# Two of three column blocks of a down projection by Strassen's seven products of quarters

## The chip, the cores and the metric

The kernel runs on one core of one Trainium2 chip. A core has a matrix engine (TensorE, "PE" in the profile, its weight loads "PEld"), VectorE ("DVE"), ScalarE ("ACT"), GpSimd ("POOL") and SyncE ("SP", which here only issues DMAs). They run side by side and meet at semaphores; each works through its own queue in order. 16 DMA engines move data between the chip's DRAM, where inputs and scratch arrays lie, and SBUF, the on-chip memory of 128 partitions. TensorE writes its results to PSUM, eight banks of 128 x 512 floats.

The metric is the device time of one execution in microseconds. Lower is better.

## What is computed

One step of a two-layer streaming encoder on 1024 prompt frames and 64 sample frames, 1088 columns in all, model width 1024, float32. Layer 0 mixes tokens by sliding-window attention, layer 1 by a diagonal state-space model (SSM). After either mixer comes the same gated feed-forward block (FFN), and the change is in its last product:

```python
def conv_ffn(h, prev, w_up, conv_w, conv_b, w_down):
    t = h.shape[1]
    up = h @ w_up                                   # 1024 -> 2 * 2816
    full = jnp.concatenate([prev.astype(up.dtype), up], axis=1)
    c = conv_b
    for j in range(CONV_WIDTH):                     # 3 taps, causal
        c = c + conv_w[j] * full[:, j:j + t]
    y = (jax.nn.gelu(c[..., :D_FF]) * c[..., D_FF:]) @ w_down   # 2816 -> 1024
    return y, full[:, -(CONV_WIDTH - 1):]
```

In each layer `x = x + rms_norm(conv_ffn(rms_norm(x)))` follows `x = x + rms_norm(mixer(rms_norm(x)))`.

## The kernel before

**Layout.** Activations are kept transposed: 128 channels on the partitions, frames along the columns. The 1088 columns fall into three blocks, 384, 384 and 320 (`BLK`). The inner size 2816 of the FFN is 22 tiles of 128 (`KF`), the width 1024 is 8 (`KD`).

**Matmuls in three.** A float32 product is made of three matmuls (`mm3`, L179). Each operand is split into a high part, a rounded copy made by ACT, and a low part, the difference made by DVE; low x high, high x high and high x low are added up in PSUM.

**Weights.** `wsrc` (L42 to L50) lists all weight units in order of use. `unit` (L149) hands out the next one and asks for those after it; `load_unit` (L161) loads a unit of 128 x 1024 floats into one of two `raw` buffers through SP's queue, ACT copies it (L175) and DVE subtracts (L176) into one of six buffers with the tag `big`. A unit of `w_down` holds two k-tiles of one half of the output (`mh`).

**The FFN** (`ffn`, L288). The up stage runs over 22 gated units `f`. Each makes two tiles of `up` (rows f and 22 + f) for all three blocks out of the normed input `h`, whose high and low parts fill the four buffers `blkA` and the two `blkB`. DVE takes the results from PSUM (L311), ACT and DVE make the convolution (L319 to L321), ACT the GELU (L334), DVE the product of the two (L337), and SP stores the gated tile to the scratch array `gd` in DRAM (L338, L340). The last three tiles of `up` before the very last are made together, block by block. In layer 0 the SSM's tables are prepared beside this at low priority (`side`, L342 to L349), in part on POOL and with a table in one of the two `ypA` buffers.

The down stage takes the blocks one after another. `part` loads gated tiles back from `gd` (`gr`) and splits them into `gt` (L385 on ACT, L386 on DVE), in two groups of 12 and 10 k-tiles (`KCUT`), in the buffers that `h` had. `down` makes 4 output tiles at a time, in 4 of the 6 PSUM banks with the tag `mm`; after the first group of k-tiles ACT copies the sums into `y` (L411), after the second DVE adds to it (L413). `y` lies in `ypA` for the first two blocks and in `ypB` for the third. When a block's `y` is whole, `after` makes its post-norm beside the next block's matmuls (`post_norm`, L260): ACT squares, DVE or POOL adds (L205, L280), DVE scales (L277), with loads of the residual `xl` and stores on SP's queue. In layer 0 more follows for the SSM: the next norm's squares, added on POOL for block 0, and scaled copies in four `blkA` buffers (`ssm_bounce`, L870), which `beside` starts at block 2.

**Order.** Instructions are not placed by hand. A scheduler orders each engine's queue at build time, from the order of the program as priority and its own model of durations; `order` and `later` bend this in places. Buffers of one tag are given out again when their last reader is done.

Of the kernel before, what the change touches and what calls it, by code (L numbers as in the profile page):

```python
# [8 lines left out]
F32 = mybir.dt.float32  # L9
# [20 lines left out]
GT = [[[(4, "blkA")] * 3, [(4, "blkA"), (3, "blkB"), (3, "blkB")]]] * 2 + [[[(4, "blkA")] * 3, [(4, "blkB"), (4, "blkB"), (2, "big")]]]  # L30
# [6 lines left out]
class Core:  # L37
    def __init__(self, ctx, tc, a):
# [5 lines left out]
        for i in range(2):  # L44
            self.wsrc += [("w_up", i, m + e) for m in range(KF) for e in (0, KF)]
            self.wsrc += [("w_down", i, k, mh) for _ in range(3) for c in range(2) for mh in range(2) for k in range(KCUT[c], KCUT[c + 1], 2)]
            if i == 0:
                self.wsrc.append(None)
                self.wsrc.append(None)
                self.wsrc += [("w_glu", m + e) for m in range(KD) for e in (0, KD)]  # L50
# [110 lines left out]
    def load_unit(self, src):  # L161
        nc = self.nc
        ap = self.a[src[0]]
        raw = self.wts.tile([P, D], F32, name="raw", tag="raw", bufs=2)
# [122 lines left out]

    def ffn(self, i, h, rb, after, side=None, beside=lambda: None):  # L288
# [6 lines left out]
        gd = self.dram.tile([P, KF, T], F32, name=f"gd{i}")  # L295

# [65 lines left out]
        def part(b, c):  # L362

            t0, n = BLK[b]
            k0 = KCUT[c]
            out = {}
            if (b, c) == (0, 0):

                r0 = [self.yp.tile([P, 6, n], F32, name="gr0", tag="yp" + x, bufs=y) for x, y in (("A", 2), ("B", 1))]
                for x, r in enumerate(r0):  # L370
                    nc.sync.dma_start(r, gd[:, 6 * x:6 * x + 6, t0:t0 + n])
            for sz, tag in GT[b][c]:
# [4 lines left out]
                for j in range(0, sz, 2):  # L377
                    e = min(2, sz - j)
                    if (b, c) == (0, 0):
                        x6 = (k0 + j) % 6  # L380
                        raw = r0[(k0 + j) // 6][:, x6:x6 + e]
                    else:
                        raw = self.t4([P, e, n], "gr")
                        nc.sync.dma_start(raw, gd[:, k0 + j:k0 + j + e, t0:t0 + n])
                    nc.scalar.activation(x[:, 0, j:j + e], raw, AF.Copy)  # L385
                    nc.vector.tensor_sub(x[:, 1, j:j + e], raw, x[:, 0, j:j + e].bitcast(F32))  # L386
                    for z in range(e):
                        out[k0 + j + z] = x, j + z
# [3 lines left out]
        def down(b, c, gs):  # L392
            t0, n = BLK[b]
            for mh in range(2):
                ps = [self.mm_ps() for _ in range(4)]
                ks = range(KCUT[c], KCUT[c + 1])
                ws = {k: self.unit(("w_down", i, k, mh)) for k in ks if k % 2 == 0} if (b, c, mh) == (2, 1, 1) else {}
# [10 lines left out]
                for m in range(4):  # L408
                    ym = y[b][:, 4 * mh + m]
# [5 lines left out]
        y = [None] * 3  # L415
        with self.boundary():
            for b in range(3):
                y[b] = self.bt(self.yp, b, "y")
                gs = part(b, 0)
                if b == 2:  # L420
                    gs.update(part(b, 1))
                    beside()
                down(b, 0, gs)
                if b < 2:
                    gs = part(b, 1)
                down(b, 1, gs)
                if b == 2 and i == 0:
                    self.wsrc.pop(0)
                after(b, y[b])
# [847 lines left out]
```

## Time and profile before

| | us |
|---|---|
| median of 3 runs | 2331.05 (2329.19 to 2331.17) |
| the profiled execution | 2330.36 |
| its span, first to last instruction | 2328.6 |
| attention and what lies ahead of it | 0 to about 400 |
| layer 0: FFN up, down | about 400 to 923, 923 to 1198 |
| layer 1: SSM with its output product | about 1198 to 1560 |
| layer 1: FFN up, down | about 1560 to 2050, 2050 to 2314 |

The profile is one execution, recorded by the hardware. The page gives for each engine the busy time and the share of the span; the granted clock tells how fast TensorE was allowed to run (1.00 is full). A row of a stretch reads: start:end, length, then for each engine the busy time and the number of instructions, the granted clock, the mean busy share of the 16 DMA engines and GB/s moved. A row of a group reads: line, engine, operation, out<-in, shape, count | busy us in all, mean ns of one | idle time of the engine just before, and what ended it. A row of the time line reads: start, length, engine, line, operation. A row of the chain of waits reads: start, length, what the end waited for there. A row of DMAs: out<-in, issuing queue, count, size, median us from issue to landing.

### The profile page before, as it was taken

The numbers are of one execution on the slowest core, as the hardware profiler recorded it, in microseconds if no ns is written. First come the engines' busy times: TensorE is split into PE (matmuls) and PEld (weight loads), VectorE is DVE, ScalarE is ACT, GpSimd is POOL, SyncE is SP. The second block draws the span as 40 slices with busy tenths as digits, with TensorE's granted clock in tenths as the row PEclk, the third lists the DMA queues.
The fourth block names the chain that finished last, engine by engine and source line by source line (L and its number), as shares of the span: only waits on it lengthen the run. The fifth ranks groups of instructions, "written<-read, shape, count | busy, mean of one in ns | idle before, by whom it ended". The sixth has DMA issues, their size and how long they took to land.

```text
span 2328.6 us, 35802 instructions
## 1 busy us (share of the span) xinstructions
PE 2262.8 (97%) x14259; PEld 2194.2 (94%) x14259; DVE 1437.8 (62%) x2596; ACT 948.4 (41%) x1735; POOL 281.6 (12%) x284
## 2 busy tenths in 40 slices
PE   8999999999999999999969899999999999999997
PEld 7987799999999999999967799999999999999997
DVE  8677639897576766564658712587555455465454
ACT  5256756422243333554435621443222222255343
POOL 6222006000123221010000000240000000000000
PEclk9999999999999999999988899999999999999998
DMA  5000015322234444755568721242211221165652
GB/s 192 34 30 19 19 60 173 115 70 104 94 121 141 133 140 144 245 178 178 187 222 284 226 66 49 71 163 84 95 64 68 84 75 65 56 211 182 214 180 97
DMA packets 167959, 287.02 MB, mean 123 GB/s; under 512 B 22032, under 2 KB 104496, under 8 KB 167664
## 3 DMA queue, kind: packets, MB, share of 16 engines
q1 hardware_dynamic: 157440, 273.41, 36.0%
q0 software_dynamic: 2032, 6.83, 0.9%
q10 hardware_dynamic: 8320, 4.49, 0.8%
q8 instruction: 112, 1.84, 0.3%
q14 instruction: 55, 0.45, 0.1%
HBM read 214.52 MB, written 70.17 MB: 122 GB/s over the span
## 4 chain that ended last, share of the span: by engine, by line
PE 49%; DMA 4%; DVE 3%; ACT 2%; issue 1%; POOL 0%; SPq 0%; ACTq 0%; DVEq 0%; POOLq 0%
PE mm L181 13%; PE mm L183 13%; PE mm L182 13%; DMA raw<-in_w_down 2%; PE pb L181 1%; PE pb L183 1%; PE pb L182 1%; PE pa L182 1%; PE pa L183 1%; PE pa L181 1%; DMA yd<-ys 1%; DVE whl L176 1%; DVE y L277 0%; ACT whl L175 0%; DMA gr<-gd 0%
## 5 line engine op out<-in xcount | busy, mean ns | idle before, releaser
L181 PE MATMUL mm<-hl,whl 128*128 128x384 f32 (+1 forms) x2232 | 735.1, 330 | 9.2 <-ACT whl L175 7.2
L182 PE MATMUL mm<-hh,whl 128*128 128x384 f32 (+1 forms) x2232 | 735.4, 329 | 0.0
L183 PE MATMUL mm<-hh,whl 128*128 128x384 f32 (+1 forms) x2232 | 732.9, 329 | 0.6 <-DVE whl L176 0.6
L175 ACT ACTIVATE whl<-raw 128x1024 fp32r<-128x1024 f32 x256 | 269.9, 1058 | 680.8 <-PE mm L183 557.5
L176 DVE TENSOR_TENSOR whl<-raw,whl 128x1024 fp32r<-128x1024 f32 x256 | 319.1, 1249 | 238.1 <-ACT whl L175 237.7
L181 PEld LDWEIGHTS mm<-hl,whl 128*128 128x128 f32 x2232 | 420.3, 188 | 11.2 <-ACT whl L175 7.2
L183 PEld LDWEIGHTS mm<-hh,whl 128*128 128x128 f32 x2232 | 420.0, 188 | 1.5 <-DVE whl L176 1.4
L182 PEld LDWEIGHTS mm<-hh,whl 128*128 128x128 f32 x2232 | 420.6, 188 | 0.4
L181 PE MATMUL mm<-gt,whl 128*128 128x384 f32 (+1 forms) x1056 | 346.1, 328 | 2.8 <-ACT y L411 1.8
L182 PE MATMUL mm<-gt,whl 128*128 128x384 f32 (+1 forms) x1056 | 345.5, 327 | 0.0
L183 PE MATMUL mm<-gt,whl 128*128 128x384 f32 (+1 forms) x1056 | 343.2, 327 | 0.5 <-DVE whl L176 0.5
L311 DVE TENSOR_TENSOR u<-rb,mm 128x384 f32<-128x384 f32 (+1 forms) x264 | 131.9, 507 | 273.8 <-PE mm L183 273.4
L181 PEld LDWEIGHTS mm<-gt,whl 128*128 128x128 f32 x1056 | 198.2, 188 | 3.7 <-ACT y L411 2.4
L183 PEld LDWEIGHTS mm<-gt,whl 128*128 128x128 f32 x1056 | 198.0, 188 | 0.8 <-DVE whl L176 0.8
L182 PEld LDWEIGHTS mm<-gt,whl 128*128 128x128 f32 x1056 | 198.3, 188 | 0.0
L320 DVE SCALAR_TENSOR_TENSOR t<-u,ppt,t 128x1090 f32<-128x1090 f32 x88 | 121.4, 1380 | 10.9 <-ACT t L319 8.2
L321 DVE SCALAR_TENSOR_TENSOR t<-u,ppt,t 128x1090 f32<-128x1090 f32 x88 | 119.8, 1361 | 1.7
L319 ACT ACTIVATE t<-u,ppt 128x1090 f32<-128x1090 f32 x88 | 114.3, 1299 | 11.0 <-DVE t L321 5.7
L280 POOL TENSOR_TENSOR y<-y,xl 128x768 f32<-128x768 f32 (+1 forms) x16 | 30.0, 1874 | 571.6 <-DVE y L277 517.0
L334 ACT ACTIVATE t<-t 128x1090 f32<-128x1090 f32 x44 | 49.0, 1114 | 100.4 <-DVE t L321 100.4
L1110 DVE SCALAR_TENSOR_TENSOR y<-pa,ppt,sg 128x384 f32<-128x384 f32 (+1 forms) x24 | 14.1, 594 | 95.2 <-ACT sg L1109 95.2
L386 DVE TENSOR_TENSOR gt<-gr,gt 128x768 fp32r<-128x768 f32 (+2 forms) x70 | 58.0, 865 | 11.8 <-ACT gt L385 11.6
(321 smaller groups left out, 3317.9 us busy)
## 6 DMA issues: line engine op xcount, KB each, us to landing
raw<-in_w_down SPq DMA_DIRECT2D x132, 512.0 KB, 4.0
raw<-in_w_up SPq DMA_DIRECT2D x88, 512.0 KB, 3.3
gd<-t SPq DMA_DIRECT2D x44, 512.0 KB, 2.6
pm<-prm SPq DMA_DIRECT2D x32, 522.0 KB, 7.4
gr<-gd SPq DMA_DIRECT2D x28, 384.0 KB, 5.0
xl<-x SPq DMA_DIRECT2D x24, 384.0 KB, 3.8
raw<-in_w_glu SPq DMA_DIRECT2D x16, 512.0 KB, 4.4
gr<-gd SPq DMA_DIRECT2D x22, 320.0 KB, 4.4
```

The lines of the kernel that those rows point to most:

```text
L175: nc.scalar.activation(w[:, 0], raw, AF.Copy)
L176: nc.vector.tensor_sub(w[:, 1], raw, w[:, 0].bitcast(F32))
L181: nc.tensor.matmul(out, w[:, 0, sl], xl, start=start, stop=False)
L182: nc.tensor.matmul(out, w[:, 0, sl], xh, start=False, stop=False)
L183: self.last_mm = nc.tensor.matmul(out, w[:, 1, sl], xh, start=False, stop=stop)
L280: x = by[q].tensor_add(yq, yq, xs[q])
L311: nc.vector.tensor_mul(u[:, t0 + 2:t0 + 2 + np_], rb[:, t0:t0 + np_], ps[:, :np_])
L319: nc.scalar.activation(t, u[:, 0:T + 2], AF.Identity, bias=cb(m), scale=cw(0, m))
L320: nc.vector.scalar_tensor_tensor(t, u[:, 1:T + 3], cw(1, m), t, op0=ALU.mult, op1=ALU.add)
L321: nc.vector.scalar_tensor_tensor(t, u[:, 2:T + 4], cw(2, m), t, op0=ALU.mult, op1=ALU.add)
L334: nc.scalar.activation(ta, ta, AF.Gelu_apprx_tanh)
L386: nc.vector.tensor_sub(x[:, 1, j:j + e], raw, x[:, 0, j:j + e].bitcast(F32))
```

## The change

In each layer, the down product of the first two blocks is made as one product of a 2 x 2 matrix of quarters by another (Strassen's scheme in Winograd's form). The inner size is halved to two times 11 k-tiles (`KH`), the output to two halves of 512, the columns to blocks 0 and 1. Seven products of quarters stand in place of eight. The first two and the fifth use quarters of `w_down` as they are, the other four use sums of quarters; four of the seven use sums of gated quarters.

Those sums are made during the up stage, one k-tile for each gated unit: for f = 1 to 11 of weight quarters (`sums_w`, stored to `sd`), for f = 11 to 21 of gated quarters (`sums_g`, stored to `td`). Each loads its quarters through POOL's DMA queue into a buffer `jt` (one of `ypA`), makes four additions there on GpSimd, and stores the result. A weight unit of a product has up to two k-tiles of one quarter (six units for 11 k-tiles). Each product has its own 11 split gated tiles; the first product's are loaded ahead into `yp` buffers. The results are added into `y` by DVE (the first product's copied by ACT), 4 tiles for each product, 8 for the sixth. Block 0 is whole after the fifth product and block 1 after the seventh. The third block is made as before.

```diff
-GT = [[[(4, "blkA")] * 3, [(4, "blkA"), (3, "blkB"), (3, "blkB")]]] * 2 + [[[(4, "blkA")] * 3, [(4, "blkB"), (4, "blkB"), (2, "big")]]]
+GT = [[(4, "blkA")] * 3, [(4, "blkB"), (4, "blkB"), (2, "big")]]
+KH = KF // 2
+PRODUCTS = (("a", 0, 0, 0, 0), ("a", 1, 0, 1, 0), ("s", 0, 0, 1, 1), ("s", 0, 1, 0, 1), ("a", 1, 1, 1, 0), ("s", 1, 1, 0, 0), ("s", 1, 0, 1, 1))
+SUMMED = (0, 0, 1, 1, 1, 1, 0)
...
-            self.wsrc += [("w_down", i, k, mh) for _ in range(3) for c in range(2) for mh in range(2) for k in range(KCUT[c], KCUT[c + 1], 2)]
+            self.wsrc += [("w_part", i, k) + x[:3] for x in PRODUCTS for k in range(0, KH, 2)]
+            self.wsrc += [("w_down", i, k, mh) for c in range(2) for mh in range(2) for k in range(KCUT[c], KCUT[c + 1], 2)]
...
+        if src[0] == "w_part":
+
+            _, i, k, s, kc, mh = src
+            n = min(2, KH - k)
+            if s == "s":
+                ap = self.sd[:, k:k + n, kc, mh]
+            else:
+                k += KH * kc
+                ap = self.a["w_down"][i, k:k + n, :, 512 * mh:512 * mh + 512].rearrange("k p m -> p k m")
+            raw = raw[:, :512 * n]
+            self.loaded = nc.sync.dma_start(raw.rearrange("p (k m) -> p k m", k=n), ap)
+            w = self.big([P, 2, D], "whl")[:, :, :512 * n]
+            nc.scalar.activation(w[:, 0], raw, AF.Copy)
+            nc.vector.tensor_sub(w[:, 1], raw, w[:, 0].bitcast(F32))
+            return w
...
+        sd = self.sd = self.dram.tile([P, KH, 2, 2, 512], F32, name=f"sd{i}")
+        td = self.dram.tile([P, KH, 2, 2, 384], F32, name=f"td{i}")
+
+        def sums(x, q, src, dst, weights):
+
+            nc.gpsimd.dma_start(x, src)
+            a11, a12, a21, a22 = q
+            G = nc.gpsimd
+            if weights:
+                G.tensor_add(a22, a21, a22)
+                G.tensor_sub(a21, a11, a21)
+                G.tensor_sub(a11, a22, a11)
+                G.tensor_sub(a12, a12, a11)
+            else:
...
+            nc.gpsimd.dma_start(dst, x)
...
+            if f == 1:
+                jt = self.yp.tile([P, 3072], F32, name="jt", tag="ypA", bufs=2)
+            if 1 <= f <= KH:
+                sums_w(jt, f - 1)
+            if f >= KH:
+                sums_g(jt, f - KH)
...
+            for sz, tag in ((4, "blkA"), (4, "blkA"), (3, "blkB")):
+                x = self.blk.tile([P, 2, sz, 384], F32R, name="gt", tag=tag, bufs=4 if tag == "blkA" else 2)
+                for j in range(0, sz, 2):
+                    e, k = min(2, sz - j), len(out)
+                    if p == 0:
+                        raw = r0[k // 6][:, k % 6:k % 6 + e]
+                    else:
+                        raw = self.t4([P, e, 384], "gr")
+                        nc.sync.dma_start(raw, td[:, k:k + e, kc, b] if SUMMED[p] else gd[:, KH * kc + k:KH * kc + k + e, 384 * b:384 * b + 384])
+                    split_units(x, slice(j, j + e), raw)
+                    out += [(x, j + z) for z in range(e)]
+            return out
+
+        def product(p, gs, ps):
+            ws = {}
+            two = lambda ks: [(k, m) for u in ((0, 1), (2, 3)) for k in ks for m in u]
+
+            for k, m in two(range(4)) + [(k, m) for k in range(4, KH - 3) for m in range(4)] + two(range(KH - 3, KH)):
+                if k - k % 2 not in ws:
+                    ws[k] = self.unit(("w_part", i, k) + PRODUCTS[p][:3])
+                w, (x, j) = ws[k - k % 2], gs[k]
+                o = k % 2 * 512 + m * P
+                self.mm3(ps[m][:, :384], w, slice(o, o + P), x[:, 0, j], x[:, 1, j], k == 0, k == KH - 1)
+
+        def pair(y0, y1, done):
+
+            lo0, hi0, lo1, hi1 = ([y[:, j + m] for m in range(4)] for y in (y0, y1) for j in (0, 4))
+
+            ends = ([(lo1, None)], [(lo0, lo1)], [(lo1, lo1)], [(hi1, lo1)], [(hi0, hi1)], [(hi1, hi1), (lo1, lo1)], [(lo1, lo1)])
+            for p in range(7):
+                gs = operand(p)
+                ps = [self.mm_ps() for _ in range(4)]
+                product(p, gs, ps)
+                for m in range(4):
+                    for o, x in ends[p]:
+                        if x is None:
+                            nc.scalar.activation(o[m], ps[m][:, :384], AF.Copy)
+                        else:
+                            nc.vector.tensor_add(o[m], x[m], ps[m][:, :384])
+                if p in (4, 6):
+                    done(p // 6)
...
         with self.boundary():
...
+            y = [self.bt(self.yp, b, "y") for b in range(2)]
+            pair(*y, lambda b: after(b, y[b]))
+            y = self.bt(self.yp, 2, "y")
+            gs = part(0)
+            gs.update(part(1))
+            beside()
+            down(y, 0, gs)
+            down(y, 1, gs)
+            if i == 0:
+                self.wsrc.pop(0)
+            after(2, y)
```

More of the change, by code (lines that the diff above doesn't have):

```diff
@@ L162, in load_unit @@
         nc = self.nc
+        raw = self.wts.tile([P, D], F32, name="raw", tag="raw", bufs=2)
+        if src[0] == "w_part":
[12 more added lines that the diff above has]
+            return w
         ap = self.a[src[0]]
-        raw = self.wts.tile([P, D], F32, name="raw", tag="raw", bufs=2)
         if src[0] == "w_down":
@@ L360, in ffn, with split_units, operand @@
                 pass
-        def part(b, c):
-            t0, n = BLK[b]
+        def split_units(x, u, raw):
+            nc.scalar.activation(x[:, 0, u], raw, AF.Copy)
+            nc.vector.tensor_sub(x[:, 1, u], raw, x[:, 0, u].bitcast(F32))
+        def operand(p):
+            _, _, _, kc, b = PRODUCTS[p]
+            out = []
+            if p == 0:
+                r0 = [self.yp.tile([P, 6, 384], F32, name="gr0", tag="yp" + x, bufs=y) for x, y in (("A", 2), ("B", 1))]
+                for x, r in enumerate(r0):
+                    n = min(6, KH - 6 * x)
+                    nc.sync.dma_start(r[:, :n], gd[:, 6 * x:6 * x + n, :384])
+            for sz, tag in ((4, "blkA"), (4, "blkA"), (3, "blkB")):
+                x = self.blk.tile([P, 2, sz, 384], F32R, name="gt", tag=tag, bufs=4 if tag == "blkA" else 2)
+                for j in range(0, sz, 2):
+                    e, k = min(2, sz - j), len(out)
+                    if p == 0:
+                        raw = r0[k // 6][:, k % 6:k % 6 + e]
[5 more added lines that the diff above has]
+            return out
@@ L365, in part @@
+        def part(c):
+            t0, n = BLK[2]
             k0 = KCUT[c]
             out = {}
[L367 to L372, printed above, removed]
+            for sz, tag in GT[c]:
                 if tag == "big":
@@ L377, in part @@
                 for j in range(0, sz, 2):
[L378 to L387, printed above, removed]
+                    raw = self.t4([P, 2, n], "gr")
+                    nc.sync.dma_start(raw, gd[:, k0 + j:k0 + j + 2, t0:])
+                    split_units(x, slice(j, j + 2), raw)
+                    for z in range(2):
                         out[k0 + j + z] = x, j + z
@@ L390, in part, with down @@
             return out
-        def down(b, c, gs):
-            t0, n = BLK[b]
+        def down(y, c, gs):
+            n = BLK[2][1]
             for mh in range(2):
@@ L396, in down @@
                 ks = range(KCUT[c], KCUT[c + 1])
-                ws = {k: self.unit(("w_down", i, k, mh)) for k in ks if k % 2 == 0} if (b, c, mh) == (2, 1, 1) else {}
+                ws = {k: self.unit(("w_down", i, k, mh)) for k in ks if k % 2 == 0} if (c, mh) == (1, 1) else {}
                 todo = [(k, m) for m in range(4) for k in ks] if ws else [(k, m) for k in ks for m in range(4)]
@@ L408, in down @@
                 for m in range(4):
-                    ym = y[b][:, 4 * mh + m]
+                    ym = y[:, 4 * mh + m]
                     if c == 0:
@@ L413, in down @@
                         nc.vector.tensor_add(ym, ym, ps[m][:, :n])
-        y = [None] * 3
         with self.boundary():
[L417 to L429, printed above, removed]
+            y = [self.bt(self.yp, b, "y") for b in range(2)]
[9 more added lines that the diff above has]
+            after(2, y)
     def attention(self, h, rb, after):
```

12 lines of the change are left out of this document (added).

## The prediction

> **What bounds the kernel now.** I read the page first, then the busy time of each engine in stretches cut at the kernel's stages (FFN of layer 0: up 380 to 923, down 923 to 1198; layer 1: up 1560 to 2050, down 2050 to 2314).
>
> ```profile
> PE 2262.8 (97%) x14259; PEld 2194.2 (94%) x14259; DVE 1437.8 (62%) x2596; ACT 948.4 (41%) x1735; POOL 281.6 (12%) x284
> ```
> ```profile
> core 0: us, PE busy (x) PEld busy (x) DVE busy (x) ACT busy (x) POOL busy (x), PEclk, DMA share, GB/s
> 380.00:923.00 543.00, 541.57 (x3341) 539.98 (x3340) 395.52 (x823) 193.08 (x284) 111.64 (x90) 1.00 0.37 121
> 470.00:560.00 90.00, 90.00 (x548) 90.00 (x547) 82.32 (x268) 25.50 (x39) 1.23 (x1) 1.00 0.26 88
> 923.00:1015.00 92.00, 91.66 (x525) 91.34 (x524) 56.21 (x66) 45.98 (x59) 0.93 (x3) 1.00 0.65 203
> 1015.00:1108.00 93.00, 93.00 (x541) 92.93 (x540) 50.68 (x59) 42.77 (x57) 11.33 (x7) 1.00 0.58 182
> 1108.00:1198.00 90.00, 84.36 (x565) 82.29 (x563) 57.64 (x69) 38.83 (x55) 4.15 (x5) 1.00 0.50 160
> 1200.00:1326.00 126.00, 92.30 (x880) 75.44 (x880) 100.97 (x186) 73.93 (x208) 5.87 (x40) 0.82 0.88 284
> 1560.00:2050.00 490.00, 489.58 (x2973) 489.52 (x2972) 263.68 (x389) 134.51 (x200) 0.39 (x1) 1.00 0.22 77
> 2050.00:2141.00 91.00, 91.00 (x524) 91.00 (x523) 50.46 (x53) 44.32 (x55) 0.61 (x1) 1.00 0.63 203
> 2141.00:2234.00 93.00, 93.00 (x538) 92.96 (x538) 47.37 (x55) 41.89 (x54) 4.16 (x2) 1.00 0.62 193
> 2234.00:2314.00 80.00, 80.00 (x548) 79.95 (x546) 39.43 (x50) 32.69 (x46) 3.99 (x2) 1.00 0.47 151
> ```
> In both FFNs PE is busy for all but a few us at full granted clock. The down rows (one for each block of columns) show it best: 91 and 93 us of PE for the blocks of 384 in layer 1, with DVE at about half and the DMA engines at 0.63. So PE sets the time there, and a matmul left out is time gained as long as nothing else grows past PE. Only block 2 of layer 0 (1108 to 1198) has a hole, 5.6 us.
>
> **The gain.** Blocks 0 and 1 issue 2 blocks x 22 k-tiles x 8 output tiles x 3 matmuls = 1056 matmuls of 384 columns in each layer; seven products issue 7 x 11 x 4 x 3 = 924. 132 go. Price of one, start to start: 91.00 us / 524 = 0.174, 91.66 / 525 = 0.175, 93.00 / 538 = 0.173. 132 x 0.174 = 23.0 us in a layer, **46 us** in both. [...]
>
> **What each product asks of the other engines.** A product takes 132 x 0.174 = 23.0 us of PE, and needs 5 weight units of 2 k-tiles and one of 1, 11 unit tiles split in two, and 4 sums out of PSUM (8 in the sixth product; the first product's 4 copies go to ACT).
>
> ```profile
> L176 DVE TENSOR_TENSOR whl<-raw,whl 128x1024 fp32r<-128x1024 f32 x256 | 319.1, 1249 | 238.1 <-ACT whl L175 237.7
> L175 ACT ACTIVATE whl<-raw 128x1024 fp32r<-128x1024 f32 x256 | 269.9, 1058 | 680.8 <-PE mm L183 557.5 <-DMA raw<-in_w_down 96.6 <-PE mm L485 11.9
> L386 DVE TENSOR_TENSOR gt<-gr,gt 128x768 fp32r<-128x768 f32 x40 | 37.0, 953 | 2.8 <-ACT gt L385 2.7
> L385 ACT ACTIVATE gt<-gr 128x768 fp32r<-128x768 f32 x40 | 31.8, 834 | 8.6 <-DMA gr<-gd 4.4 <-PE mm L181 2.1 <-PE mm L183 2.0
> L413 DVE TENSOR_TENSOR y<-y,mm 128x384 f32<-128x384 f32 x32 | 17.0, 554 | 4.5 <-PE mm L183 4.5
> ```
> DVE: 5.5 x 1.25 + 5.5 x 0.95 + 4 x 0.55 = 14.3 us of 23.0 (before, the same count of matmuls had 5.5 units, 2.75 splits and 2 sums: 10.6). ACT: 5.5 x 1.06 + 5.5 x 0.83 = 10.4. Both lie beside PE: 0 us. The sums out of PSUM leave 2 spare banks of 6, and the order of the first 4 and last 3 k-tiles gives the first two banks 18 + 24 matmuls = 7.3 us to be emptied, against 4 x 0.55 at most; 0 us.
>
> **Supply of weights.** This is the tightest cover. A raw buffer is filled, copied by ACT, subtracted by DVE, and filled again; there are two. The chain of waits in block 2 of layer 0 shows one round, and below it the landing times in layer 1's block 1:
>
> ```profile
> 1119.59 5.16 DMA raw<-in_w_down
> ...
> 1124.83 1.07 ACT whl L175
> ...
> 1125.92 1.24 DVE whl L176
> ...
> 1127.17 4.39 DMA raw<-in_w_down
> ```
> ```profile
> DMA to landing us min/median/max: 3.7/4.1/7.1
> ```
> A round is the landing L plus 2.4, so a product's six units take (5 x (L + 2.4) + L + 1.2) / 2 = 3L + 6.6. At L = 4.1: 18.9, under 23.0; the two meet at L = 5.5. L will rise: a product moves 2.88 MB of weights and 11 x 0.197 = 2.16 MB of units, 5.04 MB, where the same matmuls before moved 2.88 + 1.08 = 3.96; share 0.63 becomes about 0.80. One end: L stays at 4.1, no cost. Other end: the row with share 0.88 and its loads.
>
> ```profile
> pm<-prm SPq DMA_DIRECT2D x32, 522.0 KB, 7.4
> gr<-gd SPq DMA_DIRECT2D x28, 384.0 KB, 5.0
> prm<-tab POOLq DMA_DIRECT2D x16, 276.0 KB, 4.7
> ```
> On the line from (0.63, 4.1) to (0.88, 7.4), 0.80 gives 6.3: 25.5 us a product, 14 x 2.5 = 35 us lost. But `pm` loads are issued in bunches and queue behind each other. 1.08 MB more at 203 GB/s / 0.63 = 320 GB/s is 3.4 us a product, 0.6 on each load: L = 4.7, 20.7 us, still covered. Operand loads stand in SP's queue ahead of weight loads and single loads reach 7.1, so I take **5 us** for both layers, near the lower end.
>
> **The sums on GpSimd.** In each layer 44 additions of 512 and 44 of 384 elements, and 44 DMAs on POOL's own queue. A round (load, four additions, store) comes with each gated unit, 490 us / 22 = 22.3 us apart (two at f = 11).
>
> ```profile
> L644 POOL TENSOR_TENSOR m<-tq,tp 128x576 f32<-128x576 f32 x8 | 9.4, 1177 | 0.6
> L641 POOL TENSOR_TENSOR m<-tq,tp 128x576 f32<-128x576 f32 x8 | 14.5, 1816 | 295.6 <-DVE w L646 150.6 <-DVE u L300 145.1
> L843 POOL DMA_DIRECT2D prm<-tab x16 | 12.4, 775 | 2.4 <-POOL tab L841 2.4
> ```
> ```profile
> 1040.03 1.84 POOL L280 TENSOR_TENSOR y<-y,xl 128x768 f32<-128x768 f32 x1 [3.35 <-ACT whl L175]
> ```
> ```profile
> 1038.06 1.22 DVE L176 TENSOR_TENSOR whl<-raw,whl 128x1024 fp32r<-128x1024 f32 x1
> 1040.04 2.91 DVE L176 TENSOR_TENSOR whl<-raw,whl 128x1024 fp32r<-128x1024 f32 x1 [0.76 <-ACT whl L175]
> ```
> I estimate 1.15 us for one addition from the undisturbed 576-element row: 88 x 1.15 + 44 x 0.78 = 135 us of POOL in 490. POOL has the room, but it isn't alone: the last two rows are the same DVE subtraction, and beside a POOL addition it took 2.91 in place of 1.22, later by nearly the whole 1.84. L641 likewise takes 1816 ns where L644, the same shape, takes 1177. So the two engines hold each other up, one whole instruction at a time. The Trainium skill (SBUF — State Buffer, "SBUF: two separate sides") says this as a rule: a DVE instruction with two SBUF inputs and a GpSimd one that reads SBUF lock the shared ports for their whole length. It speaks against the change, and these rows agree.
>
> Price: at the worst each addition costs DVE its full 1.15, 101 us in a layer. Layer 1: 264 + 101 = 365 of 490. Layer 0: 396 + 101 = 497 of 543. Tight is only 470 to 560, where DVE has 82.3 of 90: 3.6 rounds x 4 x 1.15 = 17 us against 7.7 idle leaves DVE 9 us late. PE has six banks of 24 x 0.174 = 4.2 us each, so DVE can be some 20 us late with the products before PE stops. I take 0; the other end is 9 us, once. If that cover were gone, every us late would be one of PE.
>
> **Start of the down product.** The last round of unit sums can begin only when the last gated unit is stored.
>
> ```profile
> L181 PE MATMUL mm<-gt,whl x1056: 302/336/440, 923.8 to 2313.6; 128*128 128x384 f32 x118, 128*128 128x320 f32 x58
> ```
> ```profile
> 940.89 6.29 DMA gd<-t
> ```
> Stored at 947.2; POOL's load 4.7 (like `prm<-tab`): 952; four additions of 1.0 to 1.8: 956 to 959; store 4.7: 961 to 964; `gr` load 5.0 and split 1.8: 968 to 971. The third product, the first to read sums, starts at 923.8 + 46 = 970 and needs k-tile 10 only after 96 matmuls, at 987: 15 us to spare. What waits behind it: POOL's in-order queue holds nothing that is needed sooner, but the sums' buffer is wanted by block 0's `y` for the second product's results at 970: 6 us to spare. At the same time DVE works off the last gates without a pause, and two rounds of additions fall there: 0 to 8 x 1.0 us in each layer, I take 1 each, **2 us**.
>
> **Block 0's norm**, which lay beside 93 us of block 1, comes beside the last two products, 46 us.
>
> ```profile
> L277 DVE TENSOR_TENSOR y<-y,pr 128x768 f32<-128x768 f32 x24 | 21.3, 949 | 6.7 <-PE pr L233 6.7
> L205 DVE TENSOR_TENSOR sqa<-sqa 128x768 f32<-128x768 f32 x24 | 23.2, 969 | 22.6 <-ACT sqa L203 22.3
> ```
> DVE: 2 x 14.3 + 2.2 (the sixth product's second sums) + about 10 of norm (4 x 0.95, 4 x 0.97, 2 x 0.95) = 41 of 46. Its four loads of `xl` and its stores, 3.1 MB, stand in SP's queue among the weight loads there: (2 x 5.04 + 3.1) MB at 320 GB/s is 41 us of 46, so it is in these two products that I expect most of the 5 us. On DVE, layer 0 has POOL adding squares there too, 11.3 us of POOL in the row 1015 to 1108, so up to 52 of 46: 6 us late, carried into block 2, whose row leaves DVE 32 us free. I take 0, other end 6. The 5.6 us hole of that block may close or stay: -5.6 to 0, I take 0.
>
> **Sum**, from the profiled execution's 2330.36 us (span 2328.6 and 1.8 around it; 0.7 under the median 2331.05): 2330.4 - 46 + 5 + 2 = **2291.4**.
>
> **Rivals.**
> (a) Slower than before: weight landings become the bound outright. Place: the seven products; deciding point: 14 x (3L + 6.6 - 23.0) = 46, L = 6.6. At the longest landing of the row, 7.1, a product takes 27.9 us, 14 x 4.9 = 69 lost: 2330.4 - 46 + 69 = 2353. For: the rows at share 0.88. Against: medians of 4.1 at 0.63. Chance 0.07.
> (b) The same supply, in part: L = 6, 24.6 us a product, 22 lost, and 2 at the start: 2308. Chance 0.15.
> (c) The lock between POOL and DVE reaches PE at its upper ends, 9 in the up stage of layer 0 and 16 at the two starts: 2330.4 - 46 + 5 + 25 = 2314. For: the 2.91 row. Against: PE waits for no DVE work in either up stage, and the banks cover. Chance 0.10.
> (d) The last round of sums lands 10 us later than worked out, 4 past the spare, in both layers: 2299. Chance 0.05.
> (e) It saves nothing: 924 matmuls cost what 1056 did if one took 0.174 x 8 / 7 = 0.199 us. Nothing in the rows moves the price of one shape. 2330. Chance 0.03.
>
> **How the numbers follow.** The forecast as summed has 0.60, and its time is the prediction. Low end: all costs nothing and the hole closed, 2330.4 - 46 - 5.6 = 2279. High end: the supply at its upper bound, 2330.4 - 46 + 35 = 2319; (b), (c) and (d) lie within, (a) and (e) do not. About 0.2%, 5 us, is what a measurement of this kernel can tell from no change. Faster by more: 0.60 + 0.15 + 0.10 + 0.05 = 0.90; within: (e), 0.03; slower: (a), 0.07.
>
> **What would show it.** Right: the two-block stretch falls from 184 to about 162 us in each layer, PE without idle time in it, landings of `raw` under 5.5, and up stages as long as before though DVE's L176 and L320 grow. For (a) and (b): ACT's L175 waiting for `raw` while PE waits for L175, products longer than 23 us at unchanged matmul price. For (c): PE idle before an up matmul that waits for DVE. For (d): PE idle at the third product, released through `gr<-td` or `y`. For (e): start-to-start of a 384-column matmul above 0.174. Wrong altogether would be a longer stage that no row here touches, such as the SSM between 1200 and 1326.

## The result and the profile after

| | before | after |
|---|---|---|
| median, 4 runs each on one chip | 2330.63 us (2329.19 to 2331.17) | 2346.07 us (2343.43 to 2349.30) |
| ratio, 95% interval | | 1.0071, 1.0058 to 1.0083 |
| span of the profiled execution | 2328.6 | 2344.8 |
| mean granted clock | 0.986 | 0.978 |

The change makes the kernel 0.7% slower, by 15 us, where 39 us less had been predicted. Stage lengths, from PE's first and last matmuls of each stage in the two traces (up: from the last matmul of attention or of the SSM's output product to the first of the down product):

| us | up, layer 0 | down, layer 0 | SSM | up, layer 1 | down, layer 1 | what is left |
|---|---|---|---|---|---|---|
| before | 552.8 | 273.6 | 325.7 | 527.3 | 263.5 | 14.7 |
| after | 602.5 | 248.4 | 325.2 | 539.7 | 241.1 | 16.8 |
| | +49.7 | -25.2 | -0.5 | +12.4 | -22.4 | +2.1 |

So the seven products gave 47.6 us, and the stages in which their sums are made took 62 back, 50 of them in layer 0. First the engines on the page of after, then its busy times by stretches (start:end, length, each engine's busy time and instructions, granted clock, DMA share, GB/s):

```profile
PE 2237.7 (95%) x13995; PEld 2165.0 (92%) x13995; DVE 1565.7 (67%) x2652; ACT 954.2 (41%) x1743; POOL 625.5 (27%) x548
```

```profile
core 0: us, PE busy (x) PEld busy (x) DVE busy (x) ACT busy (x) POOL busy (x), PEclk, DMA share, GB/s
380.00:973.00 593.00, 558.82 (x3343) 554.61 (x3343) 467.01 (x826) 195.80 (x285) 273.73 (x210) 0.97 0.52 174
440.00:480.00 40.00, 36.96 (x207) 36.70 (x206) 39.56 (x75) 13.02 (x20) 17.70 (x13) 0.91 0.59 210
470.00:560.00 90.00, 90.00 (x547) 90.00 (x546) 88.43 (x243) 19.81 (x30) 39.43 (x33) 1.00 0.50 180
700.00:800.00 100.00, 93.00 (x572) 92.24 (x572) 72.16 (x99) 33.18 (x46) 50.76 (x39) 0.97 0.52 169
973.00:1136.00 163.00, 162.91 (x936) 161.76 (x935) 117.78 (x150) 87.50 (x113) 30.34 (x22) 1.00 0.81 265
1575.00:2087.00 512.00, 506.55 (x3066) 505.29 (x3065) 297.86 (x406) 140.05 (x212) 144.78 (x117) 1.00 0.41 142
2087.00:2249.00 162.00, 162.00 (x930) 161.56 (x929) 113.50 (x136) 85.50 (x110) 18.51 (x14) 1.00 0.83 270
```

The two stretches with the products, 973 to 1136 and 2087 to 2249, are full: 936 matmuls in 163 us and 930 in 162 (the products need 924), 0.174 each. The loss stands in the first row. Before, 3341 matmuls of this stage kept PE busy for 541.57 us of 543; now 3343 take 558.82 of 593. PE stands still for 34 us in place of 1.4, and the same matmuls are 17 us longer busy at a mean granted clock of 0.97: stops cost twice, once as time and once as clock after them.

What ended the idle time, in the view of waits from 400 to 974 of after (engine, line, waited for: us in all, times, longest), and then PE's only row of the same kind before:

```profile
POOL jt L323 <- DMA gd<-t: 69.4, 8, 17.6
POOL jt L327 <- DMA jt<-in_w_down: 57.2, 10, 7.1
...
DVE ct L894 <- ACT tp L953: 40.8, 7, 6.9
...
PE wps L931 <- DVE kt L925: 18.0, 5, 5.9
DVE m L892 <- POOL tab L745: 15.4, 6, 4.8
...
PE wps L931 <- DVE w L745: 6.3, 3, 3.5
...
PE mm L202 <- DVE u L362: 6.1, 3, 3.0
```

```profile
PE mm L181 <- DVE hl L255: 1.0, 1, 1.0
```

Two different things make PE wait. `mm` behind `u` is an ordinary up matmul that finds no empty PSUM bank, because DVE is late in emptying them. `wps` behind `kt` and `w` is the other, and the larger: transposes for the SSM's tables, which the scheduler strews among the up matmuls in PE's queue. Their chunk goes DVE, PE, DVE, ACT, POOL, with one buffer `m` used by DVE's part and by POOL's part in turn (`DVE m` waits for POOL's `tab`; before, no wait of DVE for `tab` is listed). A transpose whose input is late stops everything behind it on PE. The four rows of PE add up to 33.4 of the 34 us, 24.3 of them at `wps`.

Layer 1 has no such tables. Its 12.4 us lie at the start of its FFN, where the time line of POOL in after shows (start, length, line, operation) a round of weight sums, load and all, ahead of the pre-norm's next steps (`hl` before it, `y` after it):

```profile
1532.54 1.01 POOL L274 TENSOR_TENSOR hl<-gx,hh 128x384 fp32r<-128x384 f32 x1
1533.51 0.79 POOL L323 DMA_DIRECT2D jt<-in_w_down  x1
1538.91 1.31 POOL L327 TENSOR_TENSOR jt<-jt 128x512 f32<-128x512 f32 x1 [4.62 <-DMA jt<-in_w_down]
1540.30 1.30 POOL L328 TENSOR_TENSOR jt<-jt 128x512 f32<-128x512 f32 x1
1541.67 2.15 POOL L329 TENSOR_TENSOR jt<-jt 128x512 f32<-128x512 f32 x1
1543.90 2.16 POOL L330 TENSOR_TENSOR jt<-jt 128x512 f32<-128x512 f32 x1
1546.36 0.57 POOL L336 DMA_DIRECT2D sd<-jt  x1 [0.30 <-POOL jt L330]
1546.95 1.86 POOL L301 TENSOR_TENSOR y<-y,xl 128x768 f32<-128x768 f32 x1
```

In the program this round stands after the second gated unit. The scheduler drew it forward to a place ahead of the stage's first matmul (1547.8), and in POOL's in-order queue it stands 13 us in front of `y`, 4.6 of them idle for a load.

### The profile page after: what moved, and what is told of

It reads as the page before. It is cut to its first block, busy times and chain, and to the rows that moved or that the text cites. A ratio compares the mean times of both kernels' runs of the same rounds, so it can differ in the third digit from the quotient of the medians.

```text
span 2344.8 us, 35755 instructions
## 1 busy us (share of the span) xinstructions
PE 2237.7 (95%) x13995; PEld 2165.0 (92%) x13995; DVE 1565.7 (67%) x2652; ACT 954.2 (41%) x1743; POOL 625.5 (27%) x548
## 4 chain that ended last, share of the span: by engine, by line
PE 44%; DMA 6%; DVE 4%; ACT 2%; POOL 1%; issue 1%; SPq 0%; ACTq 0%; DVEq 0%; POOLq 0%
PE mm L202 12%; PE mm L204 12%; PE mm L203 12%; DMA yd<-ys 2%; PE pb L202 1%; PE pb L203 1%; PE pb L204 1%; PE pa L202 1%; PE pa L203 1%; PE pa L204 1%; DMA hd<-xs 1%; DMA raw<-in_w_down 1%; ACT z L1172 0%; DVE y L301 0%; DVE whl L197 0%
## 5 line engine op out<-in xcount | busy, mean ns | idle before, releaser
L202 PEld LDWEIGHTS mm<-hl,whl 128*128 128x128 f32 x2232 | 426.0, 191 | 27.0 <-DVE hl L276 8.6
L204 PEld LDWEIGHTS mm<-hh,whl 128*128 128x128 f32 x2232 | 426.0, 191 | 1.5 <-DVE whl L197 1.4
L203 PEld LDWEIGHTS mm<-hh,whl 128*128 128x128 f32 x2232 | 426.6, 191 | 0.1
L196 ACT ACTIVATE whl<-raw 128x1024 fp32r<-128x1024 f32 x168 | 176.6, 1056 | 383.2 <-PE mm L204 298.8
L202 PE MATMUL mm<-gt,whl 128*128 128x384 f32 (+1 forms) x968 | 317.6, 328 | 1.6 <-ACT whl L196 1.5
L204 PE MATMUL mm<-gt,whl 128*128 128x384 f32 (+1 forms) x968 | 316.2, 327 | 0.7 <-DVE whl L197 0.7
L203 PE MATMUL mm<-gt,whl 128*128 128x384 f32 (+1 forms) x968 | 316.4, 327 | 0.0
L202 PEld LDWEIGHTS mm<-gt,whl 128*128 128x128 f32 x968 | 182.3, 188 | 2.8 <-ACT whl L196 1.8
L204 PEld LDWEIGHTS mm<-gt,whl 128*128 128x128 f32 x968 | 182.1, 188 | 1.0 <-DVE whl L197 1.0
L203 PEld LDWEIGHTS mm<-gt,whl 128*128 128x128 f32 x968 | 182.3, 188 | 0.0
L182 ACT ACTIVATE whl<-raw 128x1024 fp32r<-128x1024 f32 x84 | 82.9, 987 | 149.2 <-DMA raw<-sd 61.7
L372 DVE SCALAR_TENSOR_TENSOR t<-u,ppt,t 128x1090 f32<-128x1090 f32 x88 | 140.5, 1597 | 1.8
L371 DVE SCALAR_TENSOR_TENSOR t<-u,ppt,t 128x1090 f32<-128x1090 f32 x88 | 137.6, 1564 | 6.0 <-ACT t L370 3.8
L323 POOL DMA_DIRECT2D jt<-gd x22 | 15.9, 725 | 346.7 <-DMA gd<-t 177.1
```

The costliest lines, as they stand in the source:

```text
L182: nc.scalar.activation(w[:, 0], raw, AF.Copy)
L196: nc.scalar.activation(w[:, 0], raw, AF.Copy)
L202: nc.tensor.matmul(out, w[:, 0, sl], xl, start=start, stop=False)
L203: nc.tensor.matmul(out, w[:, 0, sl], xh, start=False, stop=False)
L204: self.last_mm = nc.tensor.matmul(out, w[:, 1, sl], xh, start=False, stop=stop)
L371: nc.vector.scalar_tensor_tensor(t, u[:, 1:T + 3], cw(1, m), t, op0=ALU.mult, op1=ALU.add)
```

## The experiments

One row a run; "before" is the kernel before on the same chip, and all but the first and the last are one run each. Two more runs (e13 and e14) have a table of their own below. In e1, e2, e3, e8 and e11 the products read quarters that are not summed, so their results leave the sums out.

| run | us | before | up, layer 0 | up, layer 1 | down 0 / down 1 |
|---|---|---|---|---|---|
| the change | 2346.07 | 2330.63 | 602.5 | 539.7 | 248.4 / 241.1 |
| e1_no_sums | 2275.00 | 2325.61 | 552.3 | 527.3 | 244.9 / 240.8 |
| e2_additions_only | 2356.11 | 2325.61 | 601.5 | 547.3 | 244.9 / 240.8 |
| e3_transfers_only | 2303.04 | 2325.61 | 570.3 | 529.6 | 246.8 / 241.7 |
| e4_transposes_later | 2370.96 | 2325.61 | 605.3 | 539.5 | 267.0 / 242.3 |
| e5_sums_on_dve | 2326.63 | 2328.91 | 584.0 | 539.6 | 246.1 / 241.4 |
| e6_layer1_only | 2310.11 | 2328.91 | 552.4 | 531.1 | 268.1 / 245.4 |
| e7_after_norms | 2328.71 | 2328.91 | 597.4 | 527.6 | 246.2 / 240.8 |
| e8_memsets_only | 2333.23 | 2328.91 | 596.3 | 536.3 | 244.9 / 240.8 |
| e9_rounds_one_unit_late | 2336.51 | 2324.87 | 599.7 | 531.3 | 246.6 / 241.7 |
| e11_additions_spread | 2322.93 | 2324.87 | 584.0 | 531.4 | 252.7 / 240.8 |
| e12_dve_after_norms | 2317.60 | 2324.87 | 585.5 | 532.6 | 246.6 / 240.8 |
| e15_layer1_only_again | 2304.78 | 2325.49 | 552.6 | 531.3 | 268.3 / 240.6 |

### Without the sums, and with half of them

All products on plain quarters, and no rounds:

```diff
-            if s == "s":
-                ap = self.sd[:, k:k + n, kc, mh]
...
-            if 1 <= f <= KH:
-                sums_w(jt, f - 1)
-            if f >= KH:
-                sums_g(jt, f - KH)
```

> Leaves the sums out: the products read single quarters of the weights and of the gated units, nothing is added or stored on POOL, so the outputs are not the reference's. Theory (the loss lies in the up stages, where the sums stand beside other work; the seven products gain what was forecast): both up stages return to their length before, first down matmul of layer 0 at 924 and not 974, down stages as in the changed kernel (248 and 241 us), about 2285 us. Rival (the products themselves, their loads and the norms beside them cost elsewhere): 2320 or more.

2275.0, 10 us under the forecast, and both up stages back at the lengths of before (552.3 and 527.3). The seven products alone are worth 50.6 us beside the 46 worked out, and whatever was lost belongs to the rounds. Next the rounds without their DMAs, and without their additions:

```diff
-            nc.gpsimd.dma_start(x, src)
...
-            nc.gpsimd.dma_start(dst, x)
```

> Keeps the 88 additions of each layer on POOL, on a buffer that was set to zero, without their loads and stores; the products read single quarters as in e1_no_sums, so the outputs are not the reference's. Theory lock (POOL's additions hold DVE up, and PE waits for late DVE work): L371 and L372 on DVE stay near 1.57 us against 1.37, and most of the 62 us of the up stages remains, 2325 or more. Theory transfers (POOL stands in line for its loads and stores and holds up what is behind): under 2300.

```diff
-            if weights:
-                G.tensor_add(a22, a21, a22)
...
-                G.tensor_sub(a21, a21, a22)
```

> Keeps the loads and stores of the sums on POOL's queue and leaves the additions out, so what the products read are unsummed quarters and the outputs are not the reference's. Theory lock: DVE's L371 and L372 at 1.37 us again, layer 0's up stage nearly back, under 2300. Theory transfers: 2325 or more, with POOL waiting for jt and the SSM's tables late.

Transfers alone cost 18 us in layer 0 and 2 in layer 1; additions alone cost 49 and 20. The two don't add up to the change's 50 and 12, and the run with additions alone has a flaw: with no load to wait for, the additions crowd at the start of the stage, on the norm. It shows that additions suffice for a loss of this size, not how much of the change's loss they are. It also loses by another path: what PE lacks there is an empty PSUM bank (its waits from 371 to 1000), and at `wps` it waits 2.4 us only:

```profile
PE mm L200 <- DVE u L358: 34.0, 3, 19.6
```

That transfers cost anything was no part of the prediction; PE's waits in the run with transfers alone are for the tables first, as in the change:

```profile
PE wps L921 <- DVE w L735: 7.6, 4, 3.0
PE mm L202 <- DVE hl L276: 2.0, 1, 2.0
```

### What the additions do to DVE

Memsets of about the same length on POOL, which read nothing, in place of additions and transfers:

```diff
+            for _ in range(4):
+                nc.gpsimd.memset(x, 0.0)
```

> As e2_additions_only, but in place of each addition a memset of about the same length (1424 or 1104 elements), which reads nothing from SBUF; no transfers, products of unsummed quarters, so the outputs are not the reference's. Theory lock of the ports: DVE's two additions of the convolution back at 1.37 us, up stages within 5 us of e1_no_sums (552 and 527), 2275 to 2285. Rival (POOL's fixed queue is the trouble: the SSM's tables and the norm wait behind the additions): 2325 or more, as e2.

And the additions alone, each round bound to its gated unit, to mend the flaw above:

```diff
+                self.order(G.tensor_add(a22, a21, a22), self.last_gate)
```

> Only the 88 additions a layer on POOL, without any load or store of the rounds and with all products on plain quarters (so the sums are left out of the result), and each round bound to the gated unit that it belongs to. Without additions and transfers the kernel took 2275 us (up stages 552 and 527). Theory L, the lock alone: DVE's small instructions of the SSM's tables take over 1 us each beside an addition between 400 and 600, and PE waits for DVE: up stage of layer 0 at 575 or more, 2300 or more. Theory Q, that additions hurt mostly through what they wait for in POOL's queue: up stage of layer 0 under 562, layer 1 under 530, under 2290.

By the number the memsets (2333.2) met the rival's forecast and the additions (584.0 in layer 0, 2322.9) that of the lock. But neither spread its POOL work at the start: the memsets stand in one string of 85 us, and the first seven rounds of additions without a gap from 414.7 to 453.6 (from 584 on the rounds are spread). As measurements of the change's whole loss both are inconclusive, but they show DVE beside a busy POOL. From 414 to 453, one group of DVE's small table operations in the run with additions, and the same group in the kernel before, with one more that is used below (count | busy us, mean ns | idle before):

```profile
L772 DVE SCALAR_TENSOR_TENSOR sm<-sm 128x32 f32<-128x32 f32 x14 | 13.0, 930 | 0.4
```

```profile
L676 DVE SCALAR_TENSOR_TENSOR sm<-sm 128x32 f32<-128x32 f32 x14 | 2.7, 191 | 0.3
L664 DVE TENSOR_SCALAR sm<-sm 128x32 f32<-128x32 f32 x11 | 1.9, 175 | 0.1
```

The same 14 instructions take 930 ns each in place of 191: on the mean, each waits for more than half of an addition. Beside the string of memsets, from 422 to 508, that group (now L761) keeps its 188 ns, and the convolution (L357) its 1352; it is a one-input operation (L749, L664 with 175 ns in before) that is shut out:

```profile
L749 DVE TENSOR_SCALAR sm<-sm 128x32 f32<-128x32 f32 x13 | 38.6, 2970 | 4.3 <-DMA sm<-in_s_lam 4.1
L357 DVE SCALAR_TENSOR_TENSOR t<-u,ppt,t 128x1090 f32<-128x1090 f32 x7 | 9.5, 1352 | 0.0
...
L761 DVE SCALAR_TENSOR_TENSOR sm<-sm 128x32 f32<-128x32 f32 x14 | 2.6, 188 | 0.1
```

One of the 13 took 28.9 us (the line's instructions: min/median/max ns), and PE waited for the work behind it:

```profile
L749 DVE TENSOR_SCALAR sm<-sm x18: 173/512/28885, 422.3 to 558.5; 128x32 f32<-128x32 f32 x18
```

```profile
PE mm L200 <- DVE sm L761: 27.4, 1, 27.4
```

In the change itself, where loads pace the rounds, the same group is between the two; from 600 on it is the convolution that pays. After, 400 to 600 and 600 to 920, then before, 600 to 920:

```profile
L775 DVE SCALAR_TENSOR_TENSOR sm<-sm 128x32 f32<-128x32 f32 x14 | 8.0, 570 | 0.1
```

```profile
L371 DVE SCALAR_TENSOR_TENSOR t<-u,ppt,t 128x1090 f32<-128x1090 f32 x24 | 44.6, 1860 | 0.7 <-ACT t L370 0.6
```

```profile
L320 DVE SCALAR_TENSOR_TENSOR t<-u,ppt,t 128x1090 f32<-128x1090 f32 x24 | 34.0, 1418 | 4.2 <-ACT t L319 4.1
```

### The sums on DVE

```diff
-            G = nc.gpsimd
+            G = nc.vector
```

> The same sums with the same transfers, the additions made by DVE in place of POOL. Theory lock (an addition on POOL costs DVE more than the addition itself would): 88 additions of about 0.6 us are 53 us of DVE in a layer and hold nobody else up; layer 1's up stage within 4 us of e3_transfers_only (530), layer 0's between e3's 570 and 585, in all 2303 to 2320. Rival (DVE is simply full in layer 0, whoever adds): layer 0's up stage at 600 or more, 2335 or more.

2326.6 lies between the two forecasts. 584.0 in layer 0: 18 us better than on POOL, still 31 worse than before. No addition on POOL holds DVE up here, so the lock is not the whole of it. Layer 1 doesn't move (539.6). Its part is taken up by the next runs.

### The rounds behind the norm

In the first, a round's load may not start before the norm's last step on POOL; the second has the scheme in layer 1 alone, held in the same way; the third has the sums on DVE and held.

```diff
-            nc.gpsimd.dma_start(x, src)
+            self.order(nc.gpsimd.dma_start(x, src), self.last_pool)
```

> The change as it is, only that no sum stands in POOL's queue ahead of the last POOL instruction of the norm before the up stage. Theory (layer 1's 12 us come from weight sums that were put into POOL's queue among the norm's instructions): layer 1's up stage 527 to 531 in place of 540, layer 0's still 590 to 605; 2330 to 2335 beside a kernel before at 2325.6. Rival (they come from the additions as such): up stage stays at 538 to 541.

> Layer 0's down product as before; in layer 1 the seven products, with the sums on POOL, whose transfers come in POOL's queue after the last POOL instruction of the norm ahead of the up stage. If the loss is in layer 0's overfull up stage and in layer 1's norm: layer 0 as before, layer 1's up stage at most 4 us over 527, down stage at 241; 2325.6 - 22.5 + 4 + 2 = 2309. If the additions cost PE wherever they are made: layer 1's up stage at 537 or more, 2317 or more.

> The sums on DVE in place of POOL (2326.6 us with up stages 584 and 540), and now the weight rounds held behind the norm of each FFN. If layer 1's 12 us are the norm's place in the queues, as the run with the rounds held on POOL had it: up stage of layer 1 at 528 to 530, layer 0 about 580 to 584, about 2314. If they are DVE's own load: layer 1 stays at 540, about 2327.

With the rounds held on POOL, layer 1's up stage is back at 527.6 us in the first run. In the three other runs that hold them so (e6, e15 and, in the next part, e9) it is 531.1 to 531.3, with one wait of PE of 2.0 to 2.4 us for a bank that DVE empties. So 8 to 12 of the 12 us were the place of the first rounds in POOL's queue, and 88 additions with their transfers beside the rest of that stage cost 0 to 4 us. In layer 0 only 5 of 50 us go (597.4). The scheme in layer 1 alone takes 2310.1, beside the 2309 of its expectation. On DVE and held, layer 1 takes 532.6, so that most of its stay at 539.6 above was the norm's queue too, and layer 0 stays at 585.5, where PE waits for transposes again (600 to 970):

```profile
PE wps L931 <- DVE kt L925: 15.5, 6, 4.7
PE wps L931 <- DVE u L351: 5.2, 1, 5.2
```

### How the loss of layer 0 reaches PE

First the transposes alone one turn later, so that a late input has more time:

```diff
+        yield
+        behind = self.last_mm
```

> All sums kept; in the preparation of the SSM's tables the two sets of transposes on PE (wps) come one turn after the matmul (kps) whose result DVE has to copy first. Theory (PE in its fixed order waits at these transposes for DVE, 24 us in layer 0, and loses clock after each stop): the waits of wps go, layer 0's up stage gets 25 to 35 us shorter, 2311 to 2321. Rival (DVE is too late for everything, the transposes are only where PE meets it): another wait takes their place, 2338 or more.

As a whole it got worse: 2371.0, where the rival had named 2338 or more, with 605.3 and 267.0 for up and down of layer 0. The trace says something else of the stage itself. A chunk now takes four turns of the loop in place of three, 50 us in place of 42 on the mean, and the eight no longer fit ahead of the last up matmul. That one was reached after 562 us in place of 602; the rest of the chunks comes behind it, where PE has no other work to do meanwhile:

```profile
PE kps L920 <- DVE ct L894: 29.5, 1, 29.5
```

Ahead of that, six chunks lie between 600 and 900 (seven in the change), with all the sums and their transfers in place, and DVE is busy 70 to 72 us of each 100 (68 to 72 in the change). PE doesn't stand still there at all, where the change lost 17 us and clock with it:

```profile
600.00:700.00 100.00, 100.00 (x624) 99.70 (x623) 70.26 (x102) 33.64 (x51) 29.27 (x24) 1.00 0.43 142
700.00:800.00 100.00, 100.00 (x622) 99.70 (x622) 71.11 (x100) 35.73 (x50) 48.63 (x43) 1.00 0.53 181
800.00:900.00 100.00, 100.00 (x619) 99.69 (x618) 71.56 (x100) 33.60 (x48) 49.39 (x43) 1.00 0.54 180
```

So from 600 on the loss hangs on how little time the transposes leave to their inputs: when they come some 12 us after `kps` in place of some 4, they stop nothing. How much of this is the extra turn and how much the wider spacing of the chunks, this run doesn't tell. Later transposes with all eight chunks kept beside the stage were not tried.

Then POOL's queue. A round of unit sums begins with a load that waits for the store of the gated tile (69.4 us in the waits of after), and the tables on POOL stand behind it. With the rounds held as above, and each round one unit later:

```diff
-            if f >= KH:
-                sums_g(jt, f - KH)
+            if f > KH:
+                sums_g(jt, f - 1 - KH)
```

> The kernel with the weight rounds held behind the norm (2328.7 us, up stage of layer 0 597 us), and each round of unit sums begins only when the next unit is gated, so that its load no longer waits on POOL's in-order queue for the gated tile's store (59.7 us of such waits between 600 and 900 in the changed kernel, the longest 17.6). Theory Q: from 600 us on the loss comes from this queue; behind the waiting load stand the SSM's tables, and behind these DVE, ACT and the side's transposes on PE. Between 600 and 980 PE is busy 355.6 us of 380 in the changed kernel and 379.7 in the one before, so 24 us are at stake there: up stage 575 to 580, about 2308. Rival L: the lock between the additions and DVE's instructions carries it, wherever the rounds stand: 597 and 2329, within 5.

Between 600 and 900 POOL no longer waits for the store at all, and the stage is no shorter (599.7 beside 597.4). So the wait for the store is not what makes the chain late; PE now waits mostly at another of its links (400 to 980):

```profile
PE wps L932 <- DVE w L746: 21.2, 5, 5.2
PE mm L202 <- DVE u L362: 6.3, 6, 3.6
```

What was left was to take the chain itself away from the up stage, in the changed kernel (held) and in the one before. Its chunks then run after the up matmuls:

```diff
-            if side is not None and j <= SIDE:
+            if side is not None and j < 0:
```

> The kernel with the weight rounds held behind the norm (2328.7 us, up stage of layer 0 597 us, PE stopped 40 us there), with the chunks of the SSM's tables no longer beside the up stage of layer 0 but after it; nothing is left out. Only the first, small table operations still run beside it. The whole kernel will be slower, as the tables then stand between up and down; what counts is the up stage of layer 0 against that of the kernel before with the same move. Theory S: additions on POOL make the chain DVE - POOL - DVE - transposes of the tables late, and PE stops for it; without that chain the additions lie under PE, and the up stage is at most 15 us longer than that of the kernel before with the same move (what remains is the small table operations). Rival L: the lock between additions and the convolution's own DVE work stops PE, with or without the tables: 35 us or more longer.

> The kernel before with the same move of the SSM's tables, the bench mark for the run above: up stage of layer 0 at 540 to 552 us (552.8 with the tables beside it), and the whole slower by the tables' time after it, some 30 us or more. Both theories say the same here.

Both are much slower as a whole (2487.73 and 2513.98), as the tables then stand alone ahead of the down product. The up stage tells the theories apart. Busy times of the changed kernel with the chunks moved:

```profile
600.00:700.00 100.00, 100.00 (x610) 100.00 (x609) 61.71 (x86) 26.52 (x41) 16.99 (x14) 1.00 0.34 122
700.00:800.00 100.00, 100.00 (x605) 100.00 (x604) 55.22 (x78) 26.24 (x40) 27.41 (x24) 1.00 0.38 133
800.00:900.00 100.00, 100.00 (x607) 100.00 (x606) 47.91 (x72) 21.77 (x34) 26.85 (x24) 1.00 0.35 121
```

With all the rounds in place, PE doesn't lose a microsecond between 600 and 900, at full clock; with the chunks beside it, 700 to 800 had 93.00 us of PE at 0.97 in the change. Here the end of the stage is taken at its last up matmul, since the moved chunks stand ahead of the down product:

| us from attention's last matmul to the last up matmul | tables beside | tables after |
|---|---|---|
| before | 552.3 | 530.8 |
| changed, rounds behind the norm | 597.0 | 541.9 |
| difference | 44.7 | 11.1 |

So 34 of 45 us reach PE through the chunks of the tables, and 11 by what lies ahead of them, 400 to 600, with the small table operations and the late emptying of banks (`mm` behind `u`, 5.9 us there in this run). Moving the chunks takes their work off DVE and POOL as well as their transposes off PE; that the transposes are where PE stops is read from the waits and from e4_transposes_later. The expectation had set 15 as the bound for the 11.

### A version that beats both

> The kernel of the run with the scheme in layer 1 alone and its rounds held behind the norm, timed again for an interval: 18.8 us under the kernel before in the single look, so a ratio of 0.992 with both theories; were that run a lucky one, the ratio is above 0.996.

The kernel of e6_layer1_only, with the scheme in layer 1 alone and its rounds behind the norm, in six runs: 2304.78 us (2299.19 to 2308.76) beside 2325.49, ratio 0.9909, interval 0.9894 to 0.9923. It keeps the 23 us of layer 1's down stage and pays 4 for its sums; layer 0 keeps its eight products, and its up stage is as before (552.6). Its down stage is 5 us shorter in the traces of both runs of this kernel. In this one's, 4 of the 5 us are idle time of PE in block 2, 1.7 us in place of 5.6; why the hole closed was not followed up.

## Why the prediction was wrong

**What bounds the kernel, and the gain: right.** 264 matmuls at 0.174 make 46 us; the down stages gave 47.6 with the sums and 51.4 without them (e1_no_sums beside the trace of before). The excess over 46 is in layer 0, 25.2 in place of 23.0, where block 2's hole of 5.6 us shrank to 2.2 (83.76 us of PE in the 86 from 1136 to 1222). The ratio 8 to 7 held, and rival (e) is out.

**Other engines in the products, the supply of weights, the start: covered.** DVE was busy 118 of 163 us in layer 0's two blocks and 114 of 162 in layer 1's. The landings of weights in the first of these, from the view of their buffer, had a median of 4.6 where the sum had 4.7:

```profile
DMA to landing us min/median/max: 2.7/4.6/8.5
```

The DMA share came to 0.81 for the 0.80 worked out, and PE was busy 162.91 of 163 us. Of the 7 us taken for supply and start at most 3.8 were spent: the down stages are 3.5 and 0.3 us longer with the sums than without. Rivals (a), (b) and (d) did not occur.

**The sums on GpSimd: the step that failed.** It said of DVE's lateness that "PE has six banks of 24 x 0.174 = 4.2 us each, so DVE can be some 20 us late with the products before PE stops. I take 0; the other end is 9 us, once." Rival (c) had the lock reach PE, with 9 us in the up stage of layer 0 and 16 at the two starts of the down product. The starts cost next to nothing (above), and the up stages 62 us, not all of them lock. DVE's total was not what failed: at the worst it was to grow by 101 us in a layer, and it grew by 71.5 (467.01 beside 395.52) and 34.2 (297.86 beside 263.68), though one addition took 1.55 us on the mean (272 us for 176) and not the 1.15 of the estimate. What the step missed, by size:

- The cover. Six banks did cover most of the emptying of products (`mm` behind `u`: 6.1 us in the change; crowded additions, in e2_additions_only, break through this cover too). They do not cover the transposes of the SSM's tables, which stand in PE's own queue at places fixed when the kernel was built; when their input is late, PE stops at once. 34 us with their share of lost clock, by the pair of runs without and with the tables. "PE waits for no DVE work in either up stage" was true of the trace of before but for 1.0 us behind the norm's `hl`, as the chunks came in time there, and it said nothing of how little time they had to spare.
- The price of the lock between 400 and 600. The count laid the rounds evenly over the stage and priced the lock by the addition, "each addition costs DVE its full 1.15". The rounds of weight sums stand one after the other there, and the small table operations each pay: 570 ns in place of 191 in the change. The row 470 to 560 was taken as the tight one, with DVE at 82.3 of 90; it went to 88.4 and PE kept its 90.00. PE lost just ahead of it, in 440 to 480, with DVE at 39.56 of 40. About 11 us. Most of it comes with the additions on POOL and not with their transfers: with the rounds held, PE issues 1160 matmuls from 400 to 600 when they are on POOL (e7) and 1204 when they are on DVE (e12), beside 1213 before.
- Where the scheduler puts a round. The text had a round come "with each gated unit", one every 22.3 us, and so none beside the norm. In layer 1 the first rounds were drawn forward among the norm's steps on POOL: 8 to 12 us, by the four runs with one order more, and 5 in layer 0 in the same way.
- The clock. A stop was priced at its own length. In layer 0's up stage 33 us more of standing still came with 17 us of slower matmuls.

The text weighed the Trainium skill (SBUF — State Buffer, "SBUF: two separate sides") at this step: a DVE instruction with two SBUF inputs and a GpSimd instruction that reads SBUF shut each other out for a whole instruction. The traces agree: the convolution's first step, two inputs, goes from 1.42 to 1.86 us beside the sums and stays at 1.35 beside memsets, which read nothing. The rule was in the text, and its price was put under a cover that the transposes do not have.

**What stays open.** The sums on POOL, the sums on DVE and the transfers alone each make the chain of the tables late (45, 33 and 18 us in layer 0 in all, with the runs e7, e12 and e3). At the transposes themselves (`wps`) PE waits 24.3 us in the change, 7.8 with transfers alone (e3) and 6.3 with additions alone (e11, whose rounds are spread from 584 on): neither explains it by itself, and the two together cost more than their sum. How the 34 us divide among lock, POOL's queue and DVE's load was not settled. A second buffer `m`, which would take one link out, was not tried. The 2 us after the last down matmul were not followed up.

## What to carry to other kernels

Before calling an engine's added work hidden, list every instruction on the bounding engine that waits for that engine, and ask for each what covers it: a buffer ahead covers a producer, but a side job placed in PE's in-order queue has no cover but the slack that its chain has by chance. Such slack can be given on purpose: here transposes a turn later, in chunks spaced wider, no longer stopped PE as long as they lay beside the stage. Work that is free beside one layer can cost more than it brings beside another with a side chain; apply such a change layer by layer, and bind background rounds behind the steps that share their queue, since a scheduler that finds the engine free will draw them forward.

## What the hardware showed beyond this

Beside a string of POOL memsets, which read nothing, DVE's two-input operations kept their time (1352 and 188 ns), while a one-input operation of 0.175 us took 2.97 us on the mean of 13 and 28.9 once. And after PE's stops of a few us each in layer 0, the granted clock of whole stretches fell to 0.91 and 0.97, so that 33 us more of standing still lengthened the stage by 50.
